# Retention transposes moved one chunk later, and the sample's out projection paired

## The chip, the cores and the metric

One core of one Trainium2 chip runs the whole program. The metric is device time in microseconds (us). The kernel before was timed in three runs: 4223.5, 4226.44 and 4227.94 us, median 4226.44. The engines are TensorE (PE in the profile, its weight loads PEld), VectorE (DVE), ScalarE (ACT), GpSimd (POOL) and SyncE (SP, which here only issues DMAs). All data is float32.

## The reference, cut to what matters

The program is one step of a two-layer network (model width 1024) on 128 prompt tokens and 512 sample tokens. Layer 0 mixes tokens by retention, layer 1 by windowed attention; each ends in an expert mixer (128 expert rows per token, chosen from 16384). What the change touches is the retention of the sample and the projection behind it. With 4 heads, 256 key columns, 512 value columns and 4 chunks of 128 tokens:

```python
att = einsum('bhid,bhjd->bhij', qc, kc) * dmat            # decayed scores
o = einsum('bhij,bhjv->bhiv', att, vc) + einsum('bhid,bhdv->bhiv', qc * q_dec, S)
...                                                        # forward and backward, summed
mu = mean(o, -1); var = mean(square(o - mu), -1)           # per token and head, over 512
o = (o - mu) * rsqrt(var + GN_EPS)
y = (silu(g) * o) @ w_out                                  # w_out: 2048 x 1024
xs = layer_norm(DEEPNORM_ALPHA * xs + gs1 * y)             # then the expert mixer reads xs
```

The expert mixer scores each token's query against 2 x 128 keys for 8 heads, takes the top 16 twice, and sums the chosen experts' outputs.

## The kernel before, in words

**Order.** A planner turns the program text into one in-order queue per engine. What is traced earlier has priority; the planner runs a timeline with its own instruction costs, and puts an instruction into its engine's queue when, by that timeline, its inputs and buffers are ready and no earlier-traced one is. So later-traced work fills the gaps of earlier-traced work, but on the chip each queue is then worked off in the order so fixed. Generators are woven at trace time by `mix`: each yields after a piece of work, and the one that is furthest behind its weight goes next (`run` drives a mix to its end, `chain` puts generators behind one another).

**Retention of the sample (about 358 to 865 us of the span).** `retain_sample` goes through the heads (the first one's projections exist already). For each of three heads it weaves `ret_whole` (retention of the head that is projected) with `ret_project` (q, k, v and gate of the next head: L325 and L348 are its products); the fourth `ret_whole` runs with no projection beside it. `ret_whole` walks over four chunks c. It makes the scores of chunk c+1 against all four chunks (`pairs`, L424) and their decay product on DVE (`att`, L427); then the output of chunk c in one PSUM bank `po`: four products `att` by v (L443) and four decayed queries by state (L447). Then `ret_finish`: DVE takes mean and variance from the bank (L363, L365), y = (po - mean) * gate (L367) and three small steps of a reciprocal square root; ACT does its Newton steps, nine small instructions (L183 to L185), and scales the identity by it (`diag`, L369); PE multiplies four 128x128 blocks of y by `diag`, which transposes and scales them in one product (L372); ACT copies the result into yT (L373). PSUM: the projections use four banks ("bank"), `ret_whole` three ("rec").

**The prompt's expert sum (`sparse`, about 350 to 840 us).** It is traced behind the whole retention, so it fills gaps. It takes 128 steps, two to a group: POOL gathers 128 rows of 8 KB (L817, five row buffers), DVE takes a dot product with them (L821), ACT a gelu of two columns (L823 to L826), DVE two small products (L827, L829), and DVE adds the rows to the sum (L809), which frees the row buffer.

**Out projection and scores (about 865 to 1342 us).** `out_proj` multiplies yT of some chunks by ret_w_out: for each half of the 1024 columns it loads eight tiles of 512 KB (L224, eleven buffers), and each tile serves two 128-row blocks of every chunk of the call (L228). Then DVE multiplies the bank by a gate row (L236) and adds the residual (L237); a layer norm ends the call. The gate row is made once per call by eight small transposes (L151). PSUM has three "bank" buffers in this stage. `score` makes a chunk's expert scores from its xs (L653, L658), sorts them on DVE and ends, for the three chunks that go to the dense path, in `sel` (L781). `spread` turns a `sel` into a table in DRAM: 32 groups per chunk, each with two instructions on POOL (L890), two or three on DVE, four products (L894) and a copy on ACT (L897). With order = chunks 1, 2, 3, 0: `out` of chunk 1 alone; then `out` of 2 and 3 beside the score of 1; then `out` of 0 beside the score of 2; then one long mix of the scores of 3 and 0, the prompt's attention layer and the three spreads. The spreads' buffers lie in the room that yT had.

**Dense path (from 1342 us).** 128 steps of large products (L864), which can begin when the table is written; then the rest of the program, which the change doesn't touch.

Of the kernel before, what the change touches and what calls it, by code (L numbers as in the profile page):

```python
# [52 lines left out]
def body(ctx: ExitStack, tc: tile.TileContext, xall, condT, mod_w, mod_bT, ln_g, ln_b, ret_w_in, ret_w_out,  # L53
# [188 lines left out]

    hident = const.tile([P, P], F32, name="hident")

    def ret_consts(rc, tmp):
        V.tensor_scalar(hident, ident, 0.5, None, op0=ALU.mult)
        rope = rc.tile([P, 1024], F32, name="rope")
# [110 lines left out]
        for st, out in zip(streams, got):  # L358
            st.heads.append((h, *out))

    def ret_finish(rp, h, c, po, sg, yT):
        bn = lnp.tile([P, 6], F32, name="gbn")
        V.bn_stats(bn, po)  # L363
        mv = lnp.tile([P, 2], F32, name="gmv")
        V.bn_aggr(mv, bn)  # L365
        y = rp.tile([P, 512], F32, name="y")
        V.scalar_tensor_tensor(y, po, mv[:, 0:1], sg[:, c, :], op0=ALU.subtract, op1=ALU.mult)  # L367
        diag = rp.tile([P, P], F32, name="diag")
        S.activation(diag, hident, AF.Identity, scale=rstd_of(mv[:, 1:2], scalar=True))  # L369
        p = bank()  # L370
        for j in range(4):
            PE.matmul(p[:, j * P:(j + 1) * P], y[:, j * P:(j + 1) * P], diag, start=True, stop=True)  # L372
        S.copy(yT[:, h * 4:(h + 1) * 4, c * P:(c + 1) * P], p.rearrange("p (a b) -> p a b", b=P))  # L373

    def ret_single(rp, rc, stream, yT):

        M, kd = rc[1:3]
        h, q, k_, v, sg = stream.heads.pop(0)
        p = bank()
        for d in range(2):  # L380
            PE.transpose(p[:, d * P:(d + 1) * P], k_[:, d, :], ident)
        kts = [rp.tile([P, 256], F32, name="kt", bufs=2) for _ in range(2)]
        for r in range(2):
            S.activation(kts[r], p[:, :256], AF.Identity, scale=kd[:, h, r:r + 1])
        for r, dst in ((0, o_sf), (1, o_sb)):
            st = rp.tile([P, 2, 512], F32, name=f"st{r}")
            for d in range(2):
                p = bank()
                PE.matmul(p, kts[r][:, d * P:(d + 1) * P], v[:, 0, :], start=True, stop=True)
                S.copy(st[:, d, :], p)  # L390
            nc.sync.dma_start(dst[h].rearrange("(d p) f -> p d f", p=P), st)
        po, pa = bank(), bank()
        for d in range(2):
            PE.matmul(pa[:, :P], k_[:, d, :], q[:, d, :], start=(d == 0), stop=(d == 1))
        att = rp.tile([P, P], F32, name="att", bufs=2)
        V.tensor_tensor(att, pa[:, :P], M[:, h, :], op=ALU.mult)
        PE.matmul(po, att, v[:, 0, :], start=True, stop=True, skip_group_check=True)
        yield
        ret_finish(rp, h, 0, po, sg, yT)

    def ret_whole(rp, rc, stream, yT):

# [17 lines left out]
        def pairs(c):  # L420
            pa = bank()
            for j in range(n):
                for d in range(2):
                    PE.matmul(pa[:, j * P:(j + 1) * P], k_[:, d, j * P:(j + 1) * P], q[:, d, c * P:(c + 1) * P],  # L424
                              start=(d == 0), stop=(d == 1), skip_group_check=True)
            att = rp.tile([P, 4, P], F32, name="att", bufs=2)
            V.tensor_tensor(att, pa.rearrange("p (a b) -> p a b", b=P), m[:, 3 - c:7 - c, :], op=ALU.mult)  # L427
            return att

        att = pairs(0)  # L430
        yield
        for c in range(n):
            qs = []
# [11 lines left out]
            for r in range(2):  # L445
# [1 line left out]
                    PE.matmul(po, qs[r][:, d, :], st[r][:, d, :], start=False, stop=(r == 1 and d == 1),  # L447
                              skip_group_check=True)
                yield
            ret_finish(rp, h, c, po, sg, yT)  # L450
            att = nxt
            yield

    def mix(*gens):

# [325 lines left out]
            S.copy(dst, p[:, :384].rearrange("p (a b) -> p a b", b=P))  # L781

    GR = 2
    CUT = 30
    MODSPAN = 120
    RES = 2
# [2 lines left out]
    def row_tile():  # L789
        return sp_pool.tile([P, 2 * D], F32, name="rows", bufs=ROWS)  # L790

    def sparse(i, s, x, sel, y=None, cut=0):
        ei, w = sel
        h2 = sp_pool.tile([P, D], F32, name="h2")
        with tc.high_priority():
# [13 lines left out]
                    V.scalar_tensor_tensor(acc, rows[j][:, D:], co[:, j:j + 1], acc, op0=ALU.mult, op1=ALU.add)  # L809

        for g in range(NSLOT // GR):
            rows = []
            a = sp_pool.tile([P, GR], F32, name="a", bufs=3)
            for j in range(GR):
# [15 lines left out]
            if prev:  # L830
                accumulate(*prev)
            prev = (g, rows, co)
            if g + 1 == cut:
                accumulate(*prev)
                prev = None
                yield
# [233 lines left out]
    with tc.tile_pool(name="wp", bufs=3, reuse_waits="tile", side="right") as wp:  # L1070
        with ExitStack() as es:
# [40 lines left out]

            def retain_sample():
                for h in range(3):
                    yield from mix((21, aside(ret_whole(rp, rc, sample, yT), "rec")),
                                   (13, ret_project(wp, rc, h, [sample])))
                yield from aside(ret_whole(rp, rc, sample, yT), "rec")

# [9 lines left out]
    with banks(bank=3, aside=2, sc=2), tc.tile_pool(name="pk", bufs=1, reuse_waits="tile", side="right") as pk, \  # L1128
# [9 lines left out]
            late.append(peer_prompt(Packed(), wp, 1, xp1, psel))  # L1138
            yield from take(8, late[0])

        def out(c):
            return out_proj(wp, 0, 1, [yT[:, :, c * P:(c + 1) * P]], 16, ret_w_out, [xs[c]], lambda j: xs[c])

        def score(c):
            if c in X[0]:
# [2 lines left out]

        def spread(bp, c):
            o = X[0].index(c) * P  # L1150
            yield from aside(scatter(bp, bp, sl.pop(0), dn0[1][:, :, o:o + P, :]), "sc")

        order = X[0] + Y[0]
        go(out(order[0]))
        s = [score(c) for c in order]
        run((18, chain(out(order[1]), out(order[2]))), (18, s[0]))
        run((10, out(order[3])), (18, s[1]))
        ys.close()
        with tc.tile_pool(name="bp", bufs=2, reuse_waits="tile") as bp:
            pr = prompt()  # L1160
            run((36, chain(s[2], s[3])), (40, pr), (26, chain(*(spread(bp, c) for c in X[0]))))
    dense_late(0, *dn0, pick(0, X), None)
    hd.close()
    for c in Y[0]:
# [136 lines left out]
```

## Time and profile before

| | us |
|---|---|
| three runs, median (lowest, highest) | 4226.44 (4223.5, 4227.94) |
| the profiled execution | 4227.91 |
| its span, first to last instruction | 4225.8 |
| PE busy, of the span | 3928.4 (93%) |
| DVE busy | 3154.8 (75%) |
| ACT busy | 1675.1 (40%) |
| POOL busy | 1139.7 (27%) |

The mean granted clock of TensorE over the span is 0.965 of full speed. The span and the time of the profiled execution differ by 2.1 us; this execution took 1.5 us more than the median of the three runs. A busy PE is not PE at its peak, since its products overlap: shares of busy time say where an engine is occupied, and the rows of a stage say what it waits for.

### The profile page before, as it was taken

How to read it: one execution, taken by the hardware profiler on the slowest of the kernel's cores; microseconds unless marked ns; L12 is line 12 of the kernel's file. 1: busy time of each engine (PE TensorE's matmuls, PEld its weight loads, DVE VectorE, ACT ScalarE, POOL GpSimd, SP SyncE). 2: the span in 40 equal slices, each digit the busy share in tenths (PEclk: the TensorE clock that was granted, in tenths of full speed). 3: DMA queues.
4: the chain of work that ended last, by engine and by line, in shares of the span. 5: the costliest groups of instructions: out<-in, count | busy, mean ns of one | idle time of the engine just before them, and what ended most of it. 6: DMA issues, size and time to landing. Idle time of an engine off the chain costs nothing.

```text
span 4225.8 us, 57107 instructions
## 1 busy us (share of the span) xinstructions
PE 3928.4 (93%) x20292; PEld 3265.7 (77%) x20292; DVE 3154.8 (75%) x6873; ACT 1675.1 (40%) x3934; POOL 1139.7 (27%) x902
## 2 busy tenths in 40 slices
PE   7998989689987999999999979899879999999996
PEld 4675666456977999999999956577669999999995
DVE  1128888825877898888898933666678989888899
ACT  2212232211664444444444433455534444444442
POOL 0002333200673222222222300334422222222232
PEclk8999999899998999999999989999989999999998
DMA  9978888788876898988888725457689889898885
GB/s 375 366 240 326 333 334 319 273 261 276 268 233 207 304 362 325 350 334 336 331 343 336 294 83 157 137 165 220 181 297 346 327 339 340 336 352 328 333 339 218
DMA packets 485453, 1227.84 MB, mean 291 GB/s; under 512 B 27568, under 2 KB 302640, under 8 KB 409392
## 3 DMA queue, kind: packets, MB, share of 16 engines
q1 hardware_dynamic: 411440, 687.30, 47.5%
q0 software_dynamic: 73728, 536.90, 32.7%
q8 instruction: 159, 2.61, 0.2%
q14 instruction: 126, 1.03, 0.1%
HBM read 1166.69 MB, written 57.41 MB: 290 GB/s over the span
## 4 chain that ended last, share of the span: by engine, by line
PE 50%; issue 7%; DVE 4%; DMA 3%; POOL 3%; ACT 1%; SPq 0%; POOLq 0%; DVEq 0%; ACTq 0%
PE bank L864 20%; PE acc L864 19%; POOL rows L817 3%; PE aside L653 2%; PE bank L495 2%; PE sc L894 2%; DMA rows<-keysT 1%; PE aside L228 1%; PE bank L609 1%; PE bank L591 1%; DMA v<-uv 1%; DMA wh<-attn_w_in 1%; DMA wo<-attn_w_out 0%; DMA rows<-uv,ei 0%; PE sc L609 0%
## 5 line engine op out<-in xcount | busy, mean ns | idle before, releaser
L817 POOL DMA_INDIRECT rows<-uv,ei x512 | 767.5, 1499 | 2235.6 <-DVE acc L809 1639.8
L864 PE MATMUL bank<-hH,uH 128*128 128x384 f32 x2048 | 697.1, 340 | 26.2 <-ACT uH L856 22.1
L864 PE MATMUL bank<-hH,uL 128*128 128x384 f32 x2048 | 696.5, 340 | 6.3 <-DVE uL L857 6.3
L864 PE MATMUL bank<-hL,uH 128*128 128x384 f32 x2048 | 696.5, 340 | 0.0
L821 DVE CUSTOM_DVE_ANT_0 rows<-rows,h 128x1024 f32<-128x1024 f32 x512 | 623.8, 1219 | 63.0 <-DMA rows<-uv,ei 62.6
L809 DVE SCALAR_TENSOR_TENSOR acc<-rows,co,acc 128x1024 f32<-128x1024 f32 x508 | 651.1, 1282 | 7.2
L864 PE MATMUL acc<-vH,cH 128*128 128x512 f32 x1536 | 599.4, 390 | 4.0 <-ACT cH L856 4.0
L864 PE MATMUL acc<-vL,cH 128*128 128x512 f32 x1536 | 598.9, 390 | 0.0
L864 PE MATMUL acc<-vH,cL 128*128 128x512 f32 x1536 | 528.2, 389 | 0.0
L856 ACT CAST uH<-u 128x1024 fp32r<-128x1024 f32 x256 | 269.6, 1053 | 582.7 <-PE bank L864 560.5
L857 DVE TENSOR_TENSOR uL<-u,uH 128x1024 fp32r<-128x1024 f32 x256 | 313.1, 1223 | 141.2 <-ACT uH L856 130.5
L864 PEld LDWEIGHTS bank<-hH,uH 128*128 128x128 f32 x2048 | 386.8, 189 | 37.2 <-ACT uH L856 22.7
L864 PEld LDWEIGHTS bank<-hL,uH 128*128 128x128 f32 x2048 | 386.5, 189 | 9.7
L864 PEld LDWEIGHTS bank<-hH,uL 128*128 128x128 f32 x2048 | 386.3, 189 | 7.6 <-DVE uL L857 7.6
L856 ACT CAST vH<-v 128x1024 fp32r<-128x1024 f32 x256 | 268.9, 1051 | 247.3 <-PE acc L864 235.3
L857 DVE TENSOR_TENSOR vL<-v,vH 128x1024 fp32r<-128x1024 f32 x256 | 312.8, 1222 | 66.9 <-ACT vH L856 65.9
L864 PEld LDWEIGHTS acc<-vH,cL 128*128 128x128 f32 x1536 | 288.3, 188 | 59.9
L864 PEld LDWEIGHTS acc<-vH,cH 128*128 128x128 f32 x1536 | 288.9, 188 | 54.9 <-ACT cH L856 4.7
L864 PEld LDWEIGHTS acc<-vL,cH 128*128 128x128 f32 x1536 | 288.9, 188 | 50.0
L348 PE MATMUL bank<-w,hT 128*128 128x256 f32 x1280 | 295.8, 389 | 26.1 <-DVE vg L353 14.6
L348 PEld LDWEIGHTS bank<-w,hT 128*128 128x128 f32 x1280 | 246.5, 195 | 80.3 <-DVE vg L353 17.1
L890 POOL TENSOR_SCALAR rows<-cst,sel 128x128 f32<-128x128 f32 x192 | 176.8, 930 | 479.3 <-ACT sel L781 324.8
(391 smaller groups left out, 5865.3 us busy)
## 6 DMA issues: line engine op xcount, KB each, us to landing
u<-ut SPq DMA_DIRECT2D x256, 512.0 KB, 7.6
v<-uv SPq DMA_DIRECT2D x256, 512.0 KB, 7.0
wh<-wq SPq DMA_DIRECT2D x160, 512.0 KB, 5.7
w<-ret_w_in SPq DMA_DIRECT2D x48, 1024.0 KB, 9.1
Wd<-stg SPq DMA_DIRECT2D x48, 1024.0 KB, 6.1
W<-Wd SPq DMA_DIRECT2D x32, 1536.0 KB, 11.5
yT<-mod_w SPq DMA_DIRECT2D x40, 1024.0 KB, 10.1
wo<-ret_w_out SPq DMA_DIRECT2D x80, 512.0 KB, 5.9
```

The costliest lines, as they stand in the source:

```text
L228: PE.matmul(acc[j], aTs[j][:, kk, :], w[:, k, :], start=(kk == 0), stop=(kk == nk - 1))
L348: PE.matmul(p[:, :256], st.hT[:, k, c * P:(c + 1) * P], w[:, k, :], start=(k == 0), stop=(k == KT - 1))
L495: PE.matmul(p[:, :256], hT[:, k, :], w[k], start=(k == 0), stop=(k == KT - 1))
L653: PE.matmul(p[:, :T], w[k][:, a * P:(a + 1) * P], hT[:, k, :], start=(k == 0), stop=(k == KT - 1))
L809: V.scalar_tensor_tensor(acc, rows[j][:, D:], co[:, j:j + 1], acc, op0=ALU.mult, op1=ALU.add)
L817: G.indirect_dma_start(out=r, out_offset=None, in_=uv[i], in_offset=bass.IndirectOffsetOnAxis(ap=ei[:, sl:sl + 1], axis=0))
L821: V.tensor_tensor_reduce(rows[j][:, :D], rows[j][:, :D], h2, 1.0, 0.0, ALU.mult, ALU.add, a[:, j:j + 1])
L856: S.copy(hi, x)
L857: splits.append(V.tensor_tensor(lo, x, hi.bitcast(F32), op=ALU.subtract))
L864: PE.matmul(out, x, y, start=start and n == 0, stop=stop and n == 2, skip_group_check=True)
L890: (G if t > 1 else V).tensor_scalar(ah[:, t, :], C["iota"], sel[:, 0, t0 + t:t0 + t + 1], sel[:, 2, t0 + t:t0 + t + 1], op0=ALU.is_equal, ...
L894: PE.matmul(p[:, t * P:(t + 1) * P], ah[:, t, :], bh[:, t, :], start=True, stop=True)
```

## The change

`ret_finish` is cut into `ret_norm` (statistics, y, diag) and `ret_turn` (the four transposing products and the copy). In `ret_whole` the turn of chunk c-1 is traced behind the products of chunk c and ahead of the norm of chunk c; the last turn comes behind the loop, with two more yields. y moves from a buffer of its own into the ring of `att`, which has three buffers instead of two; `diag` has two. The weight of `ret_whole` in the mix is 22 instead of 21. `ret_single` (the prompt) calls both in a row as before.

`out` takes several chunks: chunks 1 and 2 in one call and alone, then chunks 3 and 0 in one call beside the score of chunk 1. The scores of 2, 3 and 0 go into the long mix, with weight 54 where two scores had 36, and `spread` waits with empty yields until a `sel` is there. `sparse` gets a parameter `pace`, and `ret_norm` fills a list `paced`; no call passes `pace`, so `behind` is always None and the block around a group has no effect.

```diff
-    def ret_finish(rp, h, c, po, sg, yT):
+    def ret_norm(rp, c, po, sg, deep=1):
         bn = lnp.tile([P, 6], F32, name="gbn")
...
-        y = rp.tile([P, 512], F32, name="y")
-        V.scalar_tensor_tensor(y, po, mv[:, 0:1], sg[:, c, :], op0=ALU.subtract, op1=ALU.mult)
-        diag = rp.tile([P, P], F32, name="diag")
+        y = rp.tile([P, 512], F32, name="y", tag="att" if deep > 1 else "y", bufs=3 if deep > 1 else 1)
+        paced.append(V.scalar_tensor_tensor(y, po, mv[:, 0:1], sg[:, c, :], op0=ALU.subtract, op1=ALU.mult))
+        diag = rp.tile([P, P], F32, name="diag", bufs=deep)
         S.activation(diag, hident, AF.Identity, scale=rstd_of(mv[:, 1:2], scalar=True))
+        return y, diag
+
+    def ret_turn(h, c, y, diag, yT):
         p = bank()
...
-            att = rp.tile([P, 4, P], F32, name="att", bufs=2)
+            att = rp.tile([P, 4, P], F32, name="att", bufs=3)
...
-            ret_finish(rp, h, c, po, sg, yT)
+            if normed:
+                ret_turn(h, c - 1, *normed, yT)
+            normed = ret_norm(rp, c, po, sg, 2)
             att = nxt
             yield
+        yield
+        ret_turn(h, n - 1, *normed, yT)
+        yield
...
+            behind = pace[min(int(g / PACE), len(pace)) - 1] if pace and g >= PACE else None
...
-                    yield from mix((21, aside(ret_whole(rp, rc, sample, yT), "rec")),
+                    yield from mix((22, aside(ret_whole(rp, rc, sample, yT), "rec")),
                                    (13, ret_project(wp, rc, h, [sample])))
...
-        def out(c):
-            return out_proj(wp, 0, 1, [yT[:, :, c * P:(c + 1) * P]], 16, ret_w_out, [xs[c]], lambda j: xs[c])
+        def out(*cs):
+            return out_proj(wp, 0, 1, [yT[:, :, c * P:(c + 1) * P] for c in cs], 16, ret_w_out,
+                            [xs[c] for c in cs], lambda j: xs[cs[j]])
...
             o = X[0].index(c) * P
+            while not sl:
+                yield
...
-        go(out(order[0]))
+        go(out(*order[:2]))
         s = [score(c) for c in order]
-        run((18, chain(out(order[1]), out(order[2]))), (18, s[0]))
-        run((10, out(order[3])), (18, s[1]))
+        run((10, out(*order[2:])), (18, s[0]))
...
-            run((36, chain(s[2], s[3])), (40, pr), (26, chain(*(spread(bp, c) for c in X[0]))))
+            run((54, chain(*s[1:])), (40, pr), (26, chain(*(spread(bp, c) for c in X[0]))))
```

## Rows read from the trace of the kernel before

**Rows 1.** Busy time by stage (length, then PE, PEld, DVE, ACT, POOL; clock; DMA).
```profile
358.00:788.00 430.00, 380.97 (x1432) 262.56 (x1433) 360.36 (x637) 119.50 (x437) 157.54 (x117) 0.94 0.89 328
788.00:865.00 77.00, 47.12 (x174) 29.84 (x173) 48.83 (x97) 21.02 (x71) 11.51 (x9) 0.80 0.58 216
865.00:1056.00 191.00, 181.00 (x821) 113.21 (x821) 80.68 (x374) 28.28 (x76) 0.31 (x1) 0.97 0.86 279
1056.00:1297.00 241.00, 225.04 (x1726) 206.02 (x1725) 192.38 (x874) 150.21 (x426) 157.59 (x160) 0.99 0.82 248
1297.00:1342.00 45.00, 33.70 (x235) 30.66 (x233) 43.67 (x196) 26.09 (x64) 33.65 (x32) 0.86 0.35 99
1342.00:4225.80 2883.80, 2730.60 (x14149) 2404.89 (x14149) 2342.68 (x4321) 1254.44 (x2660) 775.06 (x577) 0.97 0.79 290
```

**Rows 2.** Chain that ended last, 830 to 1345 us (start, us, what).
```profile
1331.42 7.98 POOL ah L890 x6
1344.81 5.44 DMA v<-uv
```

**Rows 3.** PE by line, 358.2 to 865.2 us (busy, mean ns; idle before).
```profile
L372 PE MATMUL rec<-diag,y 128*128 128x128 f32 x128 | 24.8, 355 | 59.0 <-ACT diag L369 59.0
```

**Rows 4.** Waits, 358 to 866 us (us in total, times, longest).
```profile
PE rec L372 <- ACT diag L369: 59.0, 11, 11.2
```

**Rows 5.** PE in order of time, last head, 788 to 865 us.
```profile
788.06 1.05 PE L372 MATMUL rec<-diag,y 128*128 128x128 f32 x8
788.95 3.74 PE L424 MATMUL rec<-qk,qk 128*128 128x128 f32 x32
...
808.29 2.07 PE L372 MATMUL rec<-diag,y 128*128 128x128 f32 x8 [7.33 <-ACT diag L369]
810.16 3.62 PE L424 MATMUL rec<-qk,qk 128*128 128x128 f32 x16
813.57 3.66 PE L443 MATMUL rec<-vg,att 128*128 128x512 f32 x8
```

**Rows 6.** All engines in order of time, 838 to 872 us.
```profile
842.40 0.70 DVE L363 BATCH_NORM_STATS2 gbn<-rec 128x6 f32<-128x512 f32 x1 [1.23 <-PE rec L447]
843.61 0.75 DVE L367 SCALAR_TENSOR_TENSOR y<-rec,gmv,vg 128x512 f32<-128x512 f32 x1
844.83 0.20 ACT L183 ACTIVATE rs<-rs 128x1 f32<-128x1 f32 x1 [11.05 <-DVE rs L180]
847.77 0.40 ACT L369 ACTIVATE diag<-hident,rs 128x128 f32<-128x128 f32 x1
...
854.34 6.52 SPq L224 DMA_DIRECT2D wo<-ret_w_out  x7
...
858.69 0.75 DVE L367 SCALAR_TENSOR_TENSOR y<-rec,gmv,vg 128x512 f32<-128x512 f32 x1
```

**Rows 7.** DVE by line, 396.8 to 824.3 us: first to fourteenth y.
```profile
L809 DVE SCALAR_TENSOR_TENSOR acc<-rows,co,acc 128x1024 f32<-128x1024 f32 x115 | 147.5, 1282 | 1.6
L821 DVE CUSTOM_DVE_ANT_0 rows<-rows,h 128x1024 f32<-128x1024 f32 x115 | 140.2, 1220 | 49.5 <-DMA rows<-uv,ei 49.2
L367 DVE SCALAR_TENSOR_TENSOR y<-rec,gmv,vg 128x512 f32<-128x512 f32 x14 | 10.5, 747 | 0.1
```

**Rows 8.** DVE in the same stretch (length, DVE busy, clock, DMA).
```profile
396.80:824.30 427.50, 357.57 (x637) 0.93 0.88 327
```

**Rows 9.** DVE by line between y 13 and y 14, 803.4 to 824.3 us.
```profile
L821 DVE CUSTOM_DVE_ANT_0 rows<-rows,h 128x1024 f32<-128x1024 f32 x6 | 7.3, 1219 | 0.6 <-DMA rows<-uv,ei 0.6
```

**Rows 10.** PE by line, 865.2 to 1056 us: out projection, first scores.
```profile
L228 PE MATMUL bank<-wo,yT 128*128 128x512 f32 x256 | 120.6, 613 | 6.4 <-DMA wo<-ret_w_out 6.4
L653 PE MATMUL aside<-hT,wh 128*128 128x128 f32 x452 | 54.4, 275 | 0.0
```

**Rows 11.** ACT in order of time: second and third dense selection done.
```profile
1122.23 0.47 ACT L781 COPY sel<-sbank 128x384 f32<-128x384 f32 x1
...
1224.30 0.48 ACT L781 COPY sel<-sbank 128x384 f32<-128x384 f32 x1 [4.46 <-PE sbank L780]
```

More of the change, by code (lines that the diff above doesn't have):

```diff
@@ L243, in body @@
     hident = const.tile([P, P], F32, name="hident")
+    paced = []
     def ret_consts(rc, tmp):
@@ L398, in ret_single @@
         yield
-        ret_finish(rp, h, 0, po, sg, yT)
+        ret_turn(h, 0, *ret_norm(rp, 0, po, sg), yT)
     def ret_whole(rp, rc, stream, yT):
@@ L425, in pairs @@
                               start=(d == 0), stop=(d == 1), skip_group_check=True)
-            att = rp.tile([P, 4, P], F32, name="att", bufs=2)
+            att = rp.tile([P, 4, P], F32, name="att", bufs=3)
             V.tensor_tensor(att, pa.rearrange("p (a b) -> p a b", b=P), m[:, 3 - c:7 - c, :], op=ALU.mult)
             return att
-        att = pairs(0)
+        att, normed = pairs(0), None
         yield
@@ L783, in body @@
     GR = 2
+    PACE = 2.5
     CUT = 30
@@ L790, in row_tile, with sparse @@
         return sp_pool.tile([P, 2 * D], F32, name="rows", bufs=ROWS)
-    def sparse(i, s, x, sel, y=None, cut=0):
+    def sparse(i, s, x, sel, y=None, cut=0, pace=None):
         ei, w = sel
@@ L811, in sparse @@
         for g in range(NSLOT // GR):
+            behind = pace[min(int(g / PACE), len(pace)) - 1] if pace and g >= PACE else None
+            es = ExitStack()
+            if behind is not None:
+                es.enter_context(tc.issue_after(behind.ins))
             rows = []
@@ L832, in sparse @@
             prev = (g, rows, co)
+            es.close()
             if g + 1 == cut:
```

## The prediction

> **What bounds the kernel now.** I read the busy time by stage first, then the chain of waits, then PE by line inside the two stages that the change touches, and last DVE in the first of them, since PE's waits there point to it. Up to 1342 us four stages follow one another: three heads of retention with projections beside them, the fourth head alone, out projection with the first scores, and the long mix with its tail. From 1342 us to the end nothing is edited, and I count it as it is: 2884 us [rows 1]. The chain that ended last reaches the dense path through the last spread: POOL's L890, then the first load of v [rows 2]. So the change is worth what it moves the end of that spread.
>
> In retention PE comes first: it is busy 381 of 430 us and 47 of 77 us, at a mean granted clock of 0.94 and 0.80 [rows 1]. Its idle time has one large reason: 59.0 us before the transposes L372, all of it for diag, in 11 waits of up to 11.2 us [rows 3, 4]. But why is diag late? Between the first and the fourteenth y DVE is busy 357.6 of 427.5 us [rows 8], and it stands a further 49.2 us waiting for gathered rows [rows 7]: 95% of the stretch. The prompt's expert sum fills DVE's queue, and the norms stand between its steps. PE waits, but DVE sets the pace; this decides what the first half of the change can bring.
>
> **The turn one chunk later.** PE's instructions are the same (128 products L372), and so are the ACT copies, each a chunk later, where nothing but the out projection reads them. What goes is up to 59.0 us of idle time, and a part of the slow clock behind it. After the wait of 7.33 us the eight L372 and sixteen L424 took 813.57 - 808.29 = 5.3 us; the same at full clock are 0.9 (788.06 to 788.95) and half of 3.74, together 2.8 us [rows 5]. That is one level of the clock, 1.2 for 2.4 GHz, for about 2.5 us of work; 11 times at most 27 us, and I take 20, since shorter waits lose less.
>
> What comes is a wait for PSUM. "rec" has three banks, and now pairs, po and the turn of the chunk before hold them in turn; the products of chunk c+1 (L443) need the bank that y of chunk c frees. No row shows this wait. From the end of po to the end of y is 2.0 us without expert steps in between (842.40 to 844.36) [rows 6]; with them it is the 7.33 us wait [rows 5] less the ACT part from the first step to the end of diag, 848.17 - 844.83 = 3.3 us [rows 6], so 4.0 us. Cover is the turn and the next pairs, 2.8 us. Twelve such places (three in each head): between 0 and 12 x 4 = 48 us; I take 1 us each, 12, nearest to the difference 4.0 - 2.8. Behind a waiting L443 stand all of PE's queue and, through it, the next statistics on DVE. The other new waits (att in y's ring, diag of two chunks back) hang on a turn that PE has passed before; I cost them at nothing. By PE alone the retention thus ends 59 + 20 - 12 = 67 us sooner.
>
> By DVE it is less. One expert step takes 427.5 / 115 = 3.72 us of the stretch [rows 7, 8]; 4 of the 128 steps are left when it ends. DVE has no room to go faster, so the retention ends sooner only as far as expert steps come to stand behind it in DVE's queue, and that the planner decides by its own timeline. This timeline can be read from the queue: between y 13 and y 14, in the head without projections, it put 6 steps [rows 9], 22 us at 3.72, where PE has 10 us of products (0.9 + 1.9 [rows 5], and twice 3.66, L443 and L447 being of one size). So the planner too saw PE stand some 12 us per bare chunk. With a wait of about 3 us left there, four bare chunks lose 36 us of its timeline; for the first head, whose next projections run mostly behind it, I add 15 us (an estimate). Of these 51 us the first 24 pull in the two chunks that came after the last step; the other 27 push 27 / 3.72 = 7 steps behind the retention.
>
> The chip then has to do 115 + 4 - 7 = 112 steps up to the last y, 417 us, and two more chunks' own DVE work, at most (357.6 - 147.5 - 140.2) / 14 = 5 us each [rows 7, 8]: the last y comes at 396.8 + 427 = 824 instead of 858.7 [rows 6], **35 us sooner**. With no step pushed it is 119 x 3.72 + 10 = 453, at 849: 9 us. The other end is PE's 67 us. I take 35, as the steps between y 13 and 14 speak for a planner that sees the stall. From the last y to the first product of the out projection I leave 6.5 us, as now (858.7 to 865.2): its loads wait on SP's queue for retention's state tiles (854.34 [rows 6]) in both orders. The steps pushed out fall into the out projection, where DVE is busy only 80.7 of 191 us [rows 1]; what needs their sum is the prompt's attention in the long mix, over 100 us later.
>
> **The paired out projection.** PE's products stay 256. The loads halve, from 64 to 32 tiles of 512 KB, and with them the 6.4 us for which PE waited on them [rows 10]. New: a pair takes two of three banks, the gate row the third, so a second half begins when DVE has emptied a bank. The trace has no such wait; DVE's pass over a bank is y's 0.75 us [rows 6], two passes 1.5; three places, up to 4.5 us, and 11 us if one pushed-out step stands ahead each time. I take 1.4 in all, as tiles alternate between the chunks and the first bank is done early. So -5 us, between -6 and +5.
>
> **The score that moves.** The second score was mostly in this stage: 452 - 256 = 196 of its 256 L653 [rows 10], 54.4 x 196 / 452 = 24 us, with its small products 27. Its 16 weight loads and 8 key loads leave SP's queue there and go among the attention's weights, where the DMAs are busy at 0.82 and carry 248 GB/s against 279 before [rows 1]; I cost that at nothing. In the long mix PE is busy 259 of 286 us [rows 1], so 27 us more of it cost 27 x 286 / 259 = 30. The spreads get the same 192 POOL instructions in a longer mix; their tail (45 us with PE at 34 [rows 1]) stays. Net -5 - 27 + 30: **2 us sooner**, between 12 sooner and 10 later.
>
> The list `paced` costs nothing: no call hands it on.
>
> **Sum.** 35 + 2 = 37 from the profiled execution's 4227.9 gives 4190.9; this execution was 1.5 us above the median of the runs, so 4189, and 2 us less since I took the chunks' own DVE work at its upper bound: 4187.
>
> **Rivals.**
> First, DVE alone paces: the planner leaves the expert steps where they stood. For it: DVE's 95%; against it, the 6 steps of rows 9. Gain 9 + 2: 4215. The Trainium skill (PSUM — Partial Sum Buffer, section Engine vs sequencer instructions) says that the queues of ScalarE, VectorE and GpSimd are strictly first in, first out; by that rule a norm cannot pass the steps queued ahead of it, whatever PE does, and the sum is this rival's. The trace agrees so far: DVE stood 49.2 us before dot products [rows 7] with nothing passing them.
>
> Second, PE's whole gain: enough steps (15) are pushed out. 67 + 2: 4157. Against it: a gain that large needs the planner's stalls to equal the chip's in every head, and the heads with projections had cover in its timeline.
>
> Third, slower: the long mix is held by its chain of scores. The second `sel` came at 1122, the third at 1224 [rows 11], 168 us after the mix began, and the dense path 120 us behind it. Now two scores lie ahead of the third `sel`. If they go at the pace at which one did, 168 us with 36 of 102 weights, two with 54 of 120 take 2 x 168 x 0.353 / 0.45 = 264 us, and the mix 96 us more. Against the 32 us that leave the stage before and the 35 of the retention: 29 us slower, 4255. It decides from the point where the third `sel` comes 168 + 32 + 35 = 235 us after the mix's start. Against it: successive `sel` are 102 us apart, not 168, so 200 us is likelier.
>
> Fourth, the change doesn't do what it says: the planner, which orders by its timeline, leaves the turns where PE still meets diag late on the chip, and the waits only change their name (diag to y). Within 8 us of now, 4222.
>
> **Chances and range.** The forecast 0.47; DVE alone 0.17; PE's whole gain 0.12; slower 0.12; nothing done 0.12. About 0.2% (8 us) is what a measurement can tell. The first rival lies on that border and I split it 0.11 to 0.06; of the fourth a third counts as faster. Faster 0.74, same 0.14, slower 0.12. The range 4150 to 4222 leaves out the slower case, half of the fourth and the edge of the second; the forecast alone has 4165 to 4205.
>
> **What would show it.** L372's idle before it should fall from 59 to under 15 us; L443 should show a wait on y or on a bank of about 12 us; the last y should come near 820, with some 7 dot products L821 behind it; the stage's clock should rise from 0.80. L228 should wait on wo under 2 us, the long mix should be about 316 us, and the third `sel` come about 200 us after its start. The prediction is wrong if the last y stays past 845, if more than 20 steps follow it, or if the mix grows by more than 60 us.

## The result, and the profile after

Four runs of the changed kernel have a median of 4182.89 us (4180.86 to 4184.5), beside 4225.19 for the kernel before (4223.5 to 4227.94): ratio 0.9899, 95% interval [0.9882, 0.9916], 42.3 us sooner, where 4187 was predicted. In a second sitting, beside the experiments, it ran at 4186.71 against 4218.3: ratio 0.9919 [0.9902, 0.9935]. The kernel before moved between 4213 and 4225 us from sitting to sitting, so below only ratios of one sitting are compared, or stages of profiles. The profiled execution after took 4180.86 us (span 4179.1, clock 0.97).

Busy time by stage, against [rows 1] (start:end, length, then PE, PEld, DVE, ACT and POOL, clock, DMA share, GB/s):

```profile
358.70:761.00 402.30, 369.80 (x1432) 254.89 (x1433) 340.44 (x604) 117.54 (x421) 148.38 (x109) 0.96 0.89 329
761.00:823.90 62.90, 44.98 (x174) 27.13 (x173) 51.14 (x99) 22.46 (x79) 19.47 (x16) 0.85 0.90 344
823.90:972.60 148.70, 144.32 (x535) 80.00 (x534) 52.93 (x166) 15.46 (x43) 1.80 (x1) 1.00 0.62 205
972.60:1306.60 334.00, 296.42 (x2229) 268.90 (x2227) 275.34 (x1294) 190.44 (x526) 187.28 (x192) 0.96 0.73 222
1306.60:4179.10 2872.50, 2723.82 (x14149) 2400.06 (x14149) 2343.85 (x4321) 1251.03 (x2659) 762.48 (x577) 0.98 0.79 290
```

The out projection starts 41 us sooner (865.2 to 823.9): 27 of them lie in the three heads with projections beside them, 14 in the fourth, the bare head. The out projection's stage is 42 us shorter, and the mix behind it 40 longer, since a score moved from the one to the other. This mix is counted to the first dense product, which stood at 1350.2 us before; [rows 1] end theirs at 1342, where the loads for it begin. Nothing else moved by more than 3 us.

PE in retention by line, 358.7 to 823.9 us, against [rows 3] (busy, mean ns | idle before, releaser; L372 is now L378, and L348, L443, L424 are L350, L449, L430). First two more lines of the kernel before, then the changed one:

```profile
L348 PE MATMUL bank<-w,hT 128*128 128x256 f32 x768 | 175.8, 390 | 18.4 <-DVE vg L353 14.6 <-DVE qk L331 3.8
L424 PE MATMUL rec<-qk,qk 128*128 128x128 f32 x256 | 37.7, 312 | 0.7 <-DVE mT L137 0.7
```

```profile
L350 PE MATMUL bank<-w,hT 128*128 128x256 f32 x768 | 175.8, 390 | 30.3 <-DVE vg L355 24.8 <-DVE qk L333 5.4
...
L449 PE MATMUL rec<-vg,att 128*128 128x512 f32 x128 | 59.8, 612 | 0.8 <-ACT yT L379 0.8
...
L430 PE MATMUL rec<-qk,qk 128*128 128x128 f32 x256 | 31.1, 275 | 0.7 <-DVE mT L137 0.7
L378 PE MATMUL rec<-diag,y 128*128 128x128 f32 x128 | 19.0, 297 | 19.3 <-DVE acc L821 14.0 <-ACT diag L372 5.3
```

The turns' idle time fell from 59.0 to 19.3 us, and 14.0 of what is left is one wait. Their busy time fell from 24.8 to 19.0 and that of the pairs from 37.7 to 31.1, at a granted clock that rose from 0.94 to 0.96 and, in the bare head, from 0.80 to 0.85. But the idle time before the products for v and the gate (L350, whose result goes to vg) grew by 12 us, 10 of them waits for vg. The waits of the same stretch, against [rows 4] (us in total, times, longest):

```profile
PE bank L350 <- DVE vg L355: 24.8, 2, 13.8
PE rec L378 <- DVE acc L821: 14.0, 1, 14.0
PE bank L350 <- DVE qk L333: 5.4, 1, 5.4
PE rec L378 <- ACT diag L372: 5.3, 3, 3.6
```

PE in order of time in the bare head, against [rows 5]:

```profile
784.41 3.60 PE L449 MATMUL rec<-vg,att 128*128 128x512 f32 x8
787.85 3.60 PE L453 MATMUL rec<-st,qs 128*128 128x512 f32 x8
795.05 2.07 PE L378 MATMUL rec<-diag,y 128*128 128x128 f32 x8 [3.61 <-ACT diag L372]
796.92 5.76 PE L449 MATMUL rec<-vg,att 128*128 128x512 f32 x8
...
805.95 1.05 PE L378 MATMUL rec<-diag,y 128*128 128x128 f32 x8
821.04 2.07 PE L378 MATMUL rec<-diag,y 128*128 128x128 f32 x8 [14.03 <-DVE acc L821]
823.02 1.11 PE L151 MATMUL sbank<-cst,mT 128*128 128x128 f32 x4
823.93 16.66 PE L228 MATMUL bank<-wo,yT 128*128 128x512 f32 x37
```

The turn that does not wait takes 1.05 us, those behind waits of 3.61 and 14.03 us take 2.07. The last turn has nothing behind which it could stand; DVE shows what it waits for, against [rows 6]:

```profile
813.14 0.75 DVE L370 SCALAR_TENSOR_TENSOR y<-rec,gmv,vg 128x512 f32<-128x512 f32 x1
813.80 0.14 DVE L178 TENSOR_SCALAR rs<-gmv 128x1 f32<-128x1 f32 x1
813.86 1.28 DVE L821 SCALAR_TENSOR_TENSOR acc<-rows,co,acc 128x1024 f32<-128x1024 f32 x1
815.05 0.15 DVE L179 TENSOR_SCALAR rs<-rs 128x1 int32<-128x1 int32 x1
815.12 1.22 DVE L837 CUSTOM_DVE_ANT_0 rows<-rows,h 128x1024 f32<-128x1024 f32 x1
816.26 0.08 DVE L837 DVE_READ_ACCUMULATOR2_ANT a<- 128x1 f32 x1
816.26 1.28 DVE L821 SCALAR_TENSOR_TENSOR acc<-rows,co,acc 128x1024 f32<-128x1024 f32 x1
817.46 0.15 DVE L180 TENSOR_SCALAR rs<-rs 128x1 int32<-128x1 int32 x1
```

The three instructions of 0.15 us that start the reciprocal root of the variance stand between expert steps: 3.8 us from the first's start to the last's end, before ACT can begin on diag. The profile names an expert step (acc L821) as what ended the 14.03 us, but the turn begins right behind the end of diag (820.58 to 820.98 on ACT): 6 of the 14 us pass before y starts, 4.5 from there to the end of this chain, the rest on ACT. DVE from the first to the last y, by line and as a whole, against [rows 7, 8]:

```profile
L821 DVE SCALAR_TENSOR_TENSOR acc<-rows,co,acc 128x1024 f32<-128x1024 f32 x110 | 141.0, 1281 | 1.5
L837 DVE CUSTOM_DVE_ANT_0 rows<-rows,h 128x1024 f32<-128x1024 f32 x111 | 135.3, 1221 | 37.8 <-DMA rows<-uv,ei 37.2
```

```profile
397.02:813.14 416.12, 373.66 (x1480) 260.23 (x1478) 351.92 (x635) 129.81 (x464) 147.25 (x111) 0.95 0.89 331
```

111 steps in 416.1 us are 3.75 us each, as before (3.72). In the order of DVE's queue 127 accumulating steps stood ahead of the last y; now 119. By dot products it was all 128; now 123. Before, the expert sum was over while two chunks were still to come. Behind the fourteenth y, in the kernel before, one dot product and three accumulations were left:

```profile
824.99 1.22 DVE L821 CUSTOM_DVE_ANT_0 rows<-rows,h 128x1024 f32<-128x1024 f32 x1
827.77 2.61 DVE L809 SCALAR_TENSOR_TENSOR acc<-rows,co,acc 128x1024 f32<-128x1024 f32 x2
```

So from 830.4 to the last y at 858.7 DVE had no step to do.

The out projection's stage (823.9 to 972.6 us), against [rows 10], and the later selections on ACT, against [rows 11]:

```profile
L228 PE MATMUL bank<-wo,yT 128*128 128x512 f32 x256 | 112.9, 596 | 2.4 <-DMA wo<-ret_w_out 1.7 <-ACT gb L153 0.7
L664 PE MATMUL aside<-hT,wh 128*128 128x128 f32 x224 | 26.9, 275 | 0.2 <-ACT hT L170 0.2
```

```profile
1105.56 0.48 ACT L792 COPY sel<-sbank 128x384 f32<-128x384 f32 x1 [0.89 <-PE sbank L791]
...
1204.21 0.48 ACT L792 COPY sel<-sbank 128x384 f32<-128x384 f32 x1 [0.40 <-PE sbank L791]
```

The third selection comes 232 us after the mix began (168 before), and yet the first dense product starts 102 us behind it and not 126.

### The profile page after: what moved, and what is told of

The parts are those of the page before. It is cut to its first block, busy times and chain, and to the rows that moved or that the text cites. A ratio compares the mean times of both kernels' runs of the same rounds, so it can differ in the third digit from the quotient of the medians.

```text
span 4179.1 us, 56991 instructions
## 1 busy us (share of the span) xinstructions
PE 3911.8 (94%) x20276; PEld 3250.7 (78%) x20276; DVE 3150.2 (75%) x6861; ACT 1672.5 (40%) x3930; POOL 1123.5 (27%) x902
## 4 chain that ended last, share of the span: by engine, by line
PE 67%; issue 11%; DMA 9%; DVE 6%; POOL 5%; ACT 2%; SPq 0%; POOLq 0%; ACTq 0%; DVEq 0%
PE bank L881 20%; PE acc L881 19%; PE aside L664 5%; POOL rows L833 4%; PE bank L350 4%; DMA rows<-uv,ei 3%; PE bank L228 3%; PE sc L911 2%; PE bank L506 2%; PE bank L327 2%; PE bank L620 1%; DVE acc L821 1%; DMA wh<-attn_w_in 1%; DMA Wd<-stg 1%; PE aside L228 1%
## 5 line engine op out<-in xcount | busy, mean ns | idle before, releaser
L833 POOL DMA_INDIRECT rows<-uv,ei x512 | 755.9, 1476 | 2252.1 <-DVE acc L821 1662.6
L837 DVE CUSTOM_DVE_ANT_0 rows<-rows,h 128x1024 f32<-128x1024 f32 x512 | 624.4, 1221 | 54.5 <-DMA rows<-uv,ei 54.0
L821 DVE SCALAR_TENSOR_TENSOR acc<-rows,co,acc 128x1024 f32<-128x1024 f32 x508 | 651.7, 1283 | 7.3
L350 PE MATMUL bank<-w,hT 128*128 128x256 f32 x1280 | 296.5, 389 | 37.2 <-DVE vg L355 24.8
L350 PEld LDWEIGHTS bank<-w,hT 128*128 128x128 f32 x1280 | 246.7, 195 | 89.5 <-DVE vg L355 26.0
```

The source lines that it names most:

```text
L350: PE.matmul(p[:, :256], st.hT[:, k, c * P:(c + 1) * P], w[:, k, :], start=(k == 0), stop=(k == KT - 1))
L833: G.indirect_dma_start(out=r, out_offset=None, in_=uv[i], in_offset=bass.IndirectOffsetOnAxis(ap=ei[:, sl:sl + 1], axis=0))
L837: V.tensor_tensor_reduce(rows[j][:, :D], rows[j][:, :D], h2, 1.0, 0.0, ALU.mult, ALU.add, a[:, j:j + 1])
```

## The experiments

Three times read from each profile tell the kernels' stages apart (us):

| kernel | last y | first out product | first dense product |
|---|---|---|---|
| before (again) | 858.7 (856.2) | 865.2 (862.7) | 1350.3 (1346.4) |
| after (again) | 813.1 (816.4) | 823.9 (827.2) | 1306.6 (1313.5) |
| turn only | 813.6 | 824.4 | 1308.6 |
| pairs and scores only | 859.6 | 866.0 | 1355.0 |
| turn and pairs | 815.1 | 825.9 | 1312.7 |
| after, steps paced | 794.6 | 808.3 | 1310.9 |
| old turn, pairs, steps paced | 859.9 | 872.0 | 1373.9 |
| after, no steps in retention | 766.4 | 778.0 | 1593.8 |
| after, halved steps | 770.5 | 777.8 | 1258.3 |
| before, halved steps | 811.9 | 818.4 | 1295.2 |
| after, gate by chunk | 818.8 | 829.7 | 1316.5 |
| after, coefficients on ACT | 811.9 | 821.7 | 1307.3 |

Two profiles of one kernel differ by 3 us at the first out product and by up to 7 at the dense path.

**The two halves.** The turn alone: the changed kernel with one chunk per weight load and the scores as before.

```diff
-        go(out(*order[:2]))
+        go(out(order[0]))
...
-        run((10, out(*order[2:])), (18, s[0]))
+        run((18, chain(out(order[1]), out(order[2]))), (18, s[0]))
+        run((10, out(order[3])), (18, s[1]))
...
-            run((54, chain(*s[1:])), (40, pr), (26, chain(*(spread(bp, c) for c in X[0]))))
+            run((36, chain(s[2], s[3])), (40, pr), (26, chain(*(spread(bp, c) for c in X[0]))))
```

> The turn is moved one chunk later as in the change; the out projection takes one chunk per call and the scores stand as before. Theory A (DVE's queue, filled by the prompt's expert sum, paces the retention; the moved turn gains because the planner puts some of those steps behind the retention): nearly all of the gain is here, about 4186 us, out projection starting near 824. Rival C (a good part of the gain is the halved weight loads): half of it is missing, about 4204.

4185.01 us beside 4212.84, ratio 0.9932 [0.9918, 0.9945]; the out projection starts at 824.4 as in the changed kernel. A's number came, but beside a kernel before that ran 12 us sooner in this sitting than in the first: the turn alone takes off 28 us. The reverse, the kernel before with the paired loads and the moved score (the same lines the other way round, in the kernel before):

> The out projection takes two chunks per call and the scores move as in the change; the turn stays right behind its own chunk's products. Theory A, and B (see the paced kernel): 2 us less than before, about 4223, with L228 no longer waiting 6.4 us on its loads and the long mix 40 us longer. Rival C: about 4204.

4227.67 beside 4212.84, ratio 1.0036 [1.0025, 1.0048]: 15 us longer, where A expected 2 less and C over 20 less. From the first out product to the dense path it takes 489.0 us, before 485.1 and 483.7. With the turn the same stretch is 482.7 and 486.3 with both edits, 484.2 without. So by profile the second half is worth nothing that can be told from two profiles of one kernel. Of the 15 us that it cost by time alone, this stretch holds 4 to 5; the rest has no place in the profiles and stays open. The changed kernel again settles what the whole is worth:

> The changed kernel once more, beside its two halves' comparison: the turn alone took 28 us off and the pairs and scores alone added 15. A, the halves simply add: 28 - 15 = 13 us sooner than the kernel before, ratio 0.997. B, the pairs and scores cost nothing once the turn is later, and the 15 us belong to something outside the edited stages: ratio 0.990 to 0.993, 30 to 42 us sooner, as when it was first timed.

0.9919 [0.9902, 0.9935]: the halves do not add. The kernel before was also profiled in that sitting:

> The kernel before, unchanged, for a profile: its runs lay at 4213 us beside the experiments and at 4225 beside the changed kernel. A, the difference is in the stretch after the dense path's start, which nothing edits: retention's last y at 857 to 860, first dense product at 1348 to 1352, as before. B, it is in retention: the last y some 10 us sooner.

4213.73 us; the dense path starts 4 us earlier than in the first profile and the unedited rest is 10 us shorter (2865.2 against 2875.5). Nearer A: of 14 us in the span 10 lie where nothing is edited. What differs between sittings was not found.

Last of this group, the turn and the pairs without the moved score:

```diff
-        run((10, out(*order[2:])), (18, s[0]))
+        run((10, out(*order[2:])), (36, chain(s[0], s[1])))
...
-            run((54, chain(*s[1:])), (40, pr), (26, chain(*(spread(bp, c) for c in X[0]))))
+            run((36, chain(s[2], s[3])), (40, pr), (26, chain(*(spread(bp, c) for c in X[0]))))
```

> The changed kernel with the second score left in the out projection's stage: the turn and the paired loads without the moved score. Against the turn alone (stage of 189.6 us, 294.4 us from there to the dense path): the prediction's 5 us for the pairs gives a stage of 184.6, its bounds 183.6 to 194.6; the rest stays within 3 us of 294.4. Rival: with loads no longer waited for, the stage is bound by the banks that DVE empties, 190 or more. The time is that of the changed kernel within 5 us either way.

The stage took 195.1 us (825.8 to 1020.9), 4197.69 beside 4222.68, ratio 0.9947 [0.9928, 0.9966]. Its PE rows:

```profile
L228 PE MATMUL bank<-wo,yT 128*128 128x512 f32 x256 | 114.4, 600 | 3.5 <-DMA wo<-ret_w_out 2.8 <-ACT gb L153 0.7
L664 PE MATMUL aside<-hT,wh 128*128 128x128 f32 x464 | 57.3, 280 | 0.1
L669 PE MATMUL aside<-kk,pq 128*128 128x128 f32 x56 | 10.2, 287 | 6.1 <-DMA kk<-keysT 5.8
```

The rival's number came, not its reason: L228 waits for no bank. 16 more score products lie in the stage than in the turn alone (464 for 448, 2 us), and PE waits 5.8 us for keys where it waited 3.3. The pairs by themselves gain nothing in this stage. The time was expected within 5 us of the changed kernel's and is 11 to 15 us longer, though in another sitting; by the profiles 5 to 7 us lie behind the first dense product, where nothing is edited.

**Who sets retention's length.** First the list `paced` used, so that an expert step may not be issued before the y that has its turn:

```diff
-            go(sparse(0, 0, xp1, psel.pop()))
+            go(sparse(0, 0, xp1, psel.pop(), pace=paced))
```

> The changed kernel with the list handed on: the prompt's expert sum gets pace=paced, so that a group of two steps queues on DVE behind a y, and at most about 100 of the 128 steps stand ahead of the last y instead of 123. Theory A: DVE gets room, the retention becomes PE's: 404 us of products and some 20 us of waits, so the out projection starts near 783 instead of 824 and the time is about 4148; the steps left over run beside the out projection, where DVE is idle. Rival B (PE's wait for diag was itself the loss, and DVE's load was beside the point): nothing left to gain, 4183 within 8 us.

4180.02 beside 4212.84, ratio 0.9919 [0.9905, 0.9932]: the time is B's, and A's start of the out projection at 783 did not come (808.3). The last y comes 18.5 us sooner with 24 fewer steps ahead of it, 0.8 us for each and not 3.7. DVE now stands 32 us waiting for the products ahead of its statistics, while PE still waits 19.3 us for diag: each waits for the other. And the out projection's stage gives all of it back:

```profile
808.30:975.80 167.50, 151.56 (x537) 84.15 (x537) 116.70 (x268) 26.42 (x92) 36.19 (x26) 0.95 0.91 336
```

167.5 us for 148.7: PE is idle 16 us for 4, at a granted clock of 0.95 for 1.00, with DMAs at 0.91 for 0.62. Steps pushed out are moved, not removed. The same with the turn right behind its own chunk (att in two buffers, weight 21, the list handed on as above):

```diff
-            if normed:
-                ret_turn(h, c - 1, *normed, yT)
-            normed = ret_norm(rp, c, po, sg, 2)
+            ret_turn(h, c, *ret_norm(rp, c, po, sg), yT)
...
-        yield
-        ret_turn(h, n - 1, *normed, yT)
-        yield
...
```

> Paired out projection and paced expert sum, but the turn stays right behind its own chunk's products. Theory A: DVE's part of the chain shrinks, PE still waits for the chain itself (about 6 us for each of some seven chunks without projections, 42 us in all), so the out projection starts near 830 and the time is about 4188: pacing alone is worth about what the moved turn alone is worth. Rival B: PE stands at diag as long as before, about 4223.

4242.35 beside 4212.84, ratio 1.0069 [1.0055, 1.0083]: slower than either expected. The out projection starts at 872.0, 64 us behind the new turn with the same pacing.

```profile
L378 PE MATMUL rec<-diag,y 128*128 128x128 f32 x128 | 24.2, 349 | 68.6 <-ACT diag L372 68.6
```

With 30 steps fewer ahead of the last y the old turn waits longer than ever. DVE at the third y of the bare head shows why:

```profile
837.92 0.75 DVE L370 SCALAR_TENSOR_TENSOR y<-rec,gmv,vg 128x512 f32<-128x512 f32 x1
838.58 0.14 DVE L178 TENSOR_SCALAR rs<-gmv 128x1 f32<-128x1 f32 x1
838.64 1.22 DVE L832 CUSTOM_DVE_ANT_0 rows<-rows,h 128x1024 f32<-128x1024 f32 x1
...
844.60 0.14 DVE L180 TENSOR_SCALAR rs<-rs 128x1 int32<-128x1 int32 x1
```

The paced steps are let go by y and stand right behind it, between the small instructions on which diag waits: 6 us from y to the last of them. The wait for diag is a chain through two engines' queues, and each step set into it adds its length. Then all steps but two behind the last y:

```diff
-    PACE = 2.5
+    PACE = 0.01
...
-            go(sparse(0, 0, xp1, psel.pop()))
+            go(sparse(0, 0, xp1, psel.pop(), pace=paced))
```

> The changed kernel with all but two of the prompt's 128 expert steps issued behind the last y, so that DVE is nearly free in retention. A, the steps on DVE are what is left of PE's waits: PE's idle time in retention falls from 51 us to under 20, and the out projection starts at 785 to 798, which is the 67 us that the prediction allowed PE at most. B, the rest of the idle time is the kernel's own chain of gate, norm and turn: over 35 us stay, and it starts at 803 to 810. In both the sum of experts comes late for the prompt's attention, and the whole is slower than the changed kernel: 4215 to 4270.

4472.21 us, far over the expected time: from 947.9 to 1593.8 us PE is busy 333 of 646. 210.5 us of that are one wait, up to 1274 us, for an ACT copy into a row buffer (L153), which an accumulation of the expert steps (L821) let go; these went on to 1295 us. But retention was the question: the out projection starts at 778.0, below A's 785, with 16 us of PE's idle time in these two rows and none in the others:

```profile
L350 PE MATMUL bank<-w,hT 128*128 128x256 f32 x768 | 170.7, 382 | 6.1 <-DVE vg L355 6.1
...
L378 PE MATMUL rec<-diag,y 128*128 128x128 f32 x128 | 17.9, 285 | 9.8 <-ACT diag L372 9.8
```

That is 87 us sooner than before. Steps hold both a gather and DVE work; the next run halves DVE's part alone:

```diff
+        W = D // 2 if (i, s) == (0, 0) else D
...
-                    V.scalar_tensor_tensor(acc, rows[j][:, D:], co[:, j:j + 1], acc, op0=ALU.mult, op1=ALU.add)
+                    V.scalar_tensor_tensor(acc[:, :W], rows[j][:, D:D + W], co[:, j:j + 1], acc[:, :W], op0=ALU.mult,
+                                           op1=ALU.add)
...
-                V.tensor_tensor_reduce(rows[j][:, :D], rows[j][:, :D], h2, 1.0, 0.0, ALU.mult, ALU.add, a[:, j:j + 1])
+                V.tensor_tensor_reduce(rows[j][:, :W], rows[j][:, :W], h2[:, :W], 1.0, 0.0, ALU.mult, ALU.add, a[:, j:j + 1])
```

> The changed kernel with the two long DVE instructions of each of the prompt's 128 expert steps over 512 of their 1024 columns (half of that sum is left out); the gathers move the same bytes. A, DVE's time for the steps is what holds retention: a step costs some 1.3 us of DVE less, and the out projection starts at 778 to 795, near the 778 of the run without steps. B, the gathered rows hold it (the DMAs are busy at 0.89 there): it starts at 812 to 827, and DVE's wait for rows grows from 45 us to over 100.

4131.21 us; the out projection starts at 777.8, as without any steps:

```profile
358.70:777.70 419.00, 405.93 (x1595) 276.83 (x1594) 266.27 (x699) 139.93 (x502) 133.09 (x124) 0.99 0.95 363
```

```profile
L822 DVE SCALAR_TENSOR_TENSOR acc<-rows,co,acc 128x512 f32<-128x512 f32 x123 | 92.3, 750 | 2.4
L839 DVE CUSTOM_DVE_ANT_0 rows<-rows,h 128x512 f32<-128x512 f32 x124 | 84.8, 686 | 17.3 <-DMA rows<-uv,ei 17.0
```

The gathers run at 363 GB/s and do not set the length: DVE waits 17.0 us for rows where the changed kernel waited 37.2, and PE is busy 97% of the stretch. A is shown: in the changed kernel DVE's time for the steps sets the length. The same in the kernel before:

> The kernel before, with the same halved steps. A, a chunk's own chain (norm, y, diag, turn) stalls PE whether DVE is full or not: over 40 of the 59 us idle before the turns stay, and the out projection starts at 830 to 850, some 50 us behind the new turn with halved steps. B, the old turn stalled only because steps stood ahead of the norm on DVE: under 25 us stay, and it starts under 815.

```profile
L372 PE MATMUL rec<-diag,y 128*128 128x128 f32 x128 | 22.1, 327 | 27.3 <-ACT diag L369 27.3
```

4170.85 us; 27.3 us of the 59 stay, and the out projection starts at 818.4, 40.6 us behind the new turn with halved steps. Between A and B: half of the old stall went with half of DVE's work, and the new turn is worth 41 us at either load. In the kernel before, then, the two losses stand side by side: halving the steps alone starts the out projection 46.8 us sooner (865.2 to 818.4), the turn alone 40.8 (824.4), both together 87.4.

**Did the gate tile take the removed wait's place?** The gate of one head is a single tile, whose next head waits for the y of the last chunk. In four tiles:

```diff
-                out.append((st.once if a else keep).tile([P, st.n, 512], F32, name=f"vg{a}"))
+                if a:
+                    out.append([st.once.tile([P, 512], F32, name=f"vg{a}{c}") for c in range(st.n)])
+                else:
+                    out.append(keep.tile([P, st.n, 512], F32, name=f"vg{a}"))
...
```

> The changed kernel with the gate in four tiles, one for each chunk, instead of one: the next head's gate of chunk 0 then waits for the y of chunk 0 and no longer for that of chunk 3. A, the gate tile took the place of the removed wait: PE's idle time before the gate's products falls from 30 to under 12 us, the out projection starts at 805 to 812 instead of 824, the time falls by 10 to 18 us against the changed kernel. B, PE waits there only because DVE is late with everything: the idle time moves to the turns and to the pairs, the out projection starts at 820 to 826, the time is the same within 5 us.

4183.45 beside 4218.3, ratio 0.9915 [0.9902, 0.9928], as the changed kernel in that sitting.

```profile
L353 PE MATMUL bank<-w,hT 128*128 128x256 f32 x768 | 173.7, 386 | 15.8 <-DVE vg L358 10.6 <-DVE qk L333 5.2
...
L381 PE MATMUL rec<-diag,y 128*128 128x128 f32 x128 | 20.8, 316 | 38.2 <-ACT diag L375 38.2
```

The gate's wait fell from 25.6 (the changed kernel in that sitting) to 10.6 and the turns' rose from 22.4 to 38.2. B: PE waits for DVE, and the tile only says where.

**A version from this.** If DVE's time is the length, small work taken off DVE should shorten it:

```diff
-            V.tensor_tensor(a, a, w[:, g * GR:(g + 1) * GR], op=ALU.mult)
...
-            V.scalar_tensor_tensor(co, th, 1.0, a, op0=ALU.add, op1=ALU.mult)
+            if (i, s) == (0, 0):
+                for j in range(GR):
+                    k = slice(j, j + 1)
+                    S.activation(a[:, k], a[:, k], AF.Identity, scale=w[:, g * GR + j:g * GR + j + 1])
+                    S.activation(co[:, k], th[:, k], AF.Identity, scale=a[:, k], bias=a[:, k])
+            else:
+                V.tensor_tensor(a, a, w[:, g * GR:(g + 1) * GR], op=ALU.mult)
+                V.scalar_tensor_tensor(co, th, 1.0, a, op0=ALU.add, op1=ALU.mult)
```

> The changed kernel, computing all, with the two small DVE products that make each pair of expert steps' coefficients (0.157 us each, and 14 us of waits for ACT ahead of them) moved to ACT, for the prompt's first expert sum alone. A, DVE's time per step sets the retention's length: 62 pairs give back 20 to 35 us of DVE up to the last y, the queue now holds five more steps ahead of that y (17 us at the new pace); the out projection starts at 806 to 820, the time is 4 to 18 us under the changed kernel's. B, ACT becomes what the steps and the norms wait for (four short instructions more for each pair, some 70 us, in front of the norms' chain): it starts at 825 or later, and the time is no better than the changed kernel's 4183 to 4187.

4189.57 beside 4218.4, ratio 0.9925 [0.9913, 0.9938]: no better. It starts the out projection at 821.7, between A and B. DVE from the first to the last y:

```profile
L821 DVE SCALAR_TENSOR_TENSOR acc<-rows,co,acc 128x1024 f32<-128x1024 f32 x115 | 147.2, 1280 | 16.5 <-ACT co L848 14.0
L837 DVE CUSTOM_DVE_ANT_0 rows<-rows,h 128x1024 f32<-128x1024 f32 x115 | 139.6, 1219 | 42.8 <-DMA rows<-uv,ei 42.3
```

A step takes 416.05 / 115 = 3.62 us for 3.75: the wait for ACT moved from one instruction to the next and the wait for rows grew by 5. No version that beats the changed kernel was found.

## Why the prediction was right, point by point

- **DVE sets the pace.** Right for the changed kernel, and shown by the halved steps. A step costs 3.75 us after, 3.72 was used. The planner set 8 accumulations and 5 dot products behind the last y, where 7 steps were predicted, and the turns no longer wait at most chunks. For the kernel before it is half of the matter: PE's wait for the chain cost its own 41 us there, at full and at half load of DVE.
- **112 steps up to the last y** were 111 dot products, and that they agree is luck. At the fourteenth y not 4 steps were left, but one dot product and three accumulations; and 5 dot products came behind the last y, not 7. The right count with no step pushed out gives 116 x 3.72 = 432 us, a last y at 828, 30 us sooner and not 9. So the first rival (4215) was priced too low. It still fell, as steps do stand behind the last y, which came 45 us sooner; but by this count some 30 of the 45 are the two chunks that used to come after the last step, and the steps pushed out give the smaller part. No run shows that split.
- **The rule behind that rival**, from the Trainium skill (PSUM — Partial Sum Buffer, section Engine vs sequencer instructions), is that DVE's queue is strictly first in, first out. The trace agrees: the small instructions of the last norm (813.80 to 817.46) wait between steps. What changed is the order in which the queue was written.
- **35 us by retention** were 41.3 at the first out product (865.2 to 823.9). The last y came at 813, not 824: 111 steps at 3.75 are the whole stretch, and the 10 us added for two more chunks' own work on DVE were too much, since a stretch divided by its steps already holds a share of it. Against that, 6.5 us from the last y to the first out product became 10.8, by the 14 us wait of the last turn.
- **L372's idle time under 15** was 19.3 (now L378): 14.0 of it is the last turn, which has no next chunk to stand behind. The other turns wait 5.3. This place was overlooked.
- **A wait of 12 us on a bank before L443** did not come: 0.8. Products of chunk 2 began at 784.41, ahead of the y of chunk 1 at 786.90 (the same head): they did not need its bank. The step "twelve such places (three in each head)" failed. In its place 12 us came before the gate's products; the gate run shows that this too is DVE's pace and no new bound. So the term had the right size for a wrong reason.
- **PE's bound of 67 us** (59 + 20 - 12) was too small: without steps, and with halved ones, the gain is 87. Without steps it is 49 from the turns' waits (59.0 to 9.8), 12 from those of L350 (18.4 to 6.1), which the prediction left out, and 25 of busy time (427.9 to 403.3 us at a granted clock of 0.92 and 0.99).
- **The clock of the last head** rose from 0.80 to 0.85; the busy time of turns and pairs fell by 12.4 us, where 20 was taken.
- **Out projection and moved score, 2 us sooner**: 2.4 by these two profiles (485.1 to 482.7), but 1 us later by the second profile of the changed kernel. Its terms were off by 10 us each way and cancelled: the stage took 148.7 us for 159 (191 less 5 and 27), and the mix 334 for 324. (The prediction's 316 for the mix ends with the loads, as the 1342 us of [rows 1] do; the first product comes 8 us later.) 228 of the first two scores' products moved (452 to 224), not 196. L228 waits 1.7 us for wo, as said. The gain of 5 us from pairs is not there when they are run without the moved score.
- **The slower rival** came close by its own sign, the third selection at 232 us with 235 as its point, and not in time: 102 us follow it to the first dense product, and 126 did before. Its point supposed the same tail behind a later selection.

Measured alone the turn gives 28 us and the whole 32 to 42, and both start the out projection at 824 to 827. So the turn is most of the gain, and the range of 4150 to 4222 rests on that half.

## What to carry to other kernels

A wait of the busiest engine for a long chain through two other queues can be hidden behind its next piece of work. What is left then belongs to the engine that paces that chain (46 us here), and is found by halving its work and leaving the transfers alone. When one wait is taken away and another grows by as much, lift the new one by itself before calling it a bound. Where a planner writes the order, count in the queue what stands ahead of the last instruction of a stage, and where: 24 steps fewer, with the rest bunched behind each y, gave 18.5 us where 46 were left.

## What the runs showed of the hardware

Halving the columns of DVE's long instructions does not halve their time: 1281 ns became 750 and 1221 became 686, so some 220 and 150 ns do not shrink ((2 x 750 - 1281) and (2 x 686 - 1221), if the rest goes with the columns). Their cost in the queue is less than these times, since the next instruction starts before the end: in the rows of DVE above the accumulation at 816.26 has one 1.20 us behind its start, and the dot product at 815.12 one 1.14. And three DVE instructions of 0.15 us are 3.8 us of a chain when long ones stand between them.
